# A hybrid attention trunk on one core: merge gates moved between the mixers, first output units interleaved, AV read in two places, one reciprocal a head, fillers at the start, new planner durations

## The chip, the core and the metric

The kernel runs on one core of a Trainium2 chip, in one launch. The metric is the time of one execution on the device in microseconds (us), here the median of three runs. Beside the times stands one profiled execution, a record of every instruction with its start, its length and what it waited for. Engines are named as in the profile: PE is TensorE (matmuls), PEld its weight loads, DVE is VectorE, ACT is ScalarE, POOL is GpSimd, SP is SyncE, which issues the DMAs. L407 is line 407 of the kernel before the change.

## The reference

x is [1, 256, 1024] in float32. Two layers follow each other, each of this form:

```
h = rms_norm(x) * gain
proj = h @ w_in                                  # 1024 -> 9808 columns, split into the parts below
oa = moba_attention(rope(qa), rope(ka), va)      # 8 heads of 64; 256 tokens are one block: causal attention
ob = dsa_attention(rope(qb), rope(kb), vb, ...)  # keeps the 64 best keys a query by an index score
oc = forgetting_attention(qc, kc, vc, log_f)     # causal, with a bias from the sums of log_f
o* = o* * silu(g*)                               # ga, gb, gc: 512 columns each
y  = [oa @ w_branch[0], ob @ w_branch[1], oc @ w_branch[2]]
merged = sum over branches of sigmoid(merge_logit) * y     # merge_logit: 3 x 1024 columns
x = x + merged @ w_out
```

The index score of the second branch is the sum over 8 heads of w * relu(q_idx . k_idx). After the layers comes one last RMS norm. Rotary embedding turns the first 16 of the 64 columns of a head.

## The kernel before, in words

**Precision.** Every float32 operand of a matmul is split into a high part (rounded to the fp32r format) and a low part, the rest. A product of two numbers then takes three matmuls: high by high, low by high, high by low. Weights come from DRAM in chunks of up to 1 MB (`raw`, 3 buffers) and are split in pieces of 128x1024: ACT writes the high part `wh` (L362), DVE the low part `wl` (L366), 6 buffers of each. Activations are split in the same way: `hTh`/`hTl` is the normalised, transposed input of a layer, `og0h`/`og0l` and `og1h`/`og1l` are gated branch outputs, `v` is the value operand and later, in the same space, the merged activations.

**Units.** The projections are cut into units, each with one bank of PSUM (`proj`, 3 banks). All their matmuls stand at L407. `unit_b` makes 128 output columns for all 256 tokens from 8 chunks of the input width: 24 matmuls of 256 moving columns. Two units in a row share one 1 MB chunk and its two split pieces. `unit_a` makes 128 tokens by 512 output columns: 24 matmuls of 512 moving columns (values, output projection); its weights are four pieces, `gets[0]` to `gets[3]`, each for two of the eight chunks. `unit_y` is the branch projection, 12 matmuls of 256; two units share one piece. Their names: q, g, k with branch letter and pair (`qa0`), `va0`, `vc0` for values, `qi0` to `qi3` for the index queries, `m20` for merge gate 0 of branch c (n = 0, 1, 2 are branches a, b, c), `y20` for its branch projection, `o00` to `o11` for the output projection (half of the columns, tile of tokens).

**Order of a layer.** Values of a, then the index key, then the index queries and mixer a, with merge gates between their units; values of c and mixer c with branch projections of a and merge gates; values of b and mixer b with branch projections of c and merge gates; the rest of b's merge gates; b's branch projections; the output projection. `between(main, fill)` spreads pairs of `fill` units evenly behind pairs of `main` units; `alternate(a, b)` takes pairs in turn. NC1 says how many of c's eight merge gates stand beside mixer a, NB1 how many of b's stand beside mixer b. All matmuls of units carry one token (`k_main`), so PE runs the units exactly in the written order.

**Attention.** A mixer has four pairs of heads. When a pair's q and k are done, `attend` runs: scores (6 matmuls, L574 to L576), for each head and each of the two query tiles a masked maximum (DVE, L637), an exponential with its sum (ACT, L641), a reciprocal of the sum (DVE, L645) and the normalising (DVE or ACT, L649/L652), then three transposes a head (L664), the split of the transposed weights (ACT L667, DVE L669) and AV, four matmuls a head (L679 to L682). AV's output goes through `gated` (ACT L695, DVE L697, product with the gate on DVE L700) and is split again (L397, L398). With the index scores done, `select` finds the 64 best keys by eight rounds of top-8 and replace on DVE (L808, L809).

**Token order.** Units read their moving operand in turns, one column from the first half of the tokens and one from the second (`turns`). Before the change AV reads its moving operand in plain order.

**Planner.** No engine's order is written by hand. At build time `Plan.run` simulates the five queues with a duration for each operation (`t_act`, `t_dve`, `t_pool`, `t_mm` and additions such as HALF) and delays between engines (LAG). It repeatedly takes the engine that can start next, and of the operations ready there the one with the lowest key. Keys are the numbers of the units, so that an earlier unit's work goes first; split pieces carry a key 2 lower than their unit (SPLIT_LEAD). The order so found is fixed in the program, and each engine runs its queue strictly in that order. Durations thus never change what is computed, only the order and which of two engines does an operation that has two ways.

**Start and end.** Fourteen matmuls of ones by ones (L870) run first on PE. `first_v` (L955) makes the values of a in layer 0, both tiles of tokens mixed, as the weights arrive. At the very end `forms` (L1048 to L1077) issues 28 matmuls whose results nobody reads, with several ways to read the moving operand.

Of the kernel before, what the change touches and what calls it, by code (L numbers as in the profile page):

```python
# [15 lines left out]
S = 256  # L16
# [23 lines left out]
HALF = 95.0  # L40
# [4 lines left out]
NC1 = 4  # L45
DMA_KEY = (-95, -94, -85, -84)
HI_KEY = (-60, -48, -47, -46)
NB1 = 2
# [186 lines left out]
def hybrid_trunk(ctx, tc, x, norm_gain, w_in, forget_bias, w_branch, w_out, final_gain, consts, out):  # L235
# [109 lines left out]
    def piece(key, ckey, ap, cshape, sel, shape, k):  # L345
# [21 lines left out]
        act(hi, a * b, False, [c], [p[0]], k - SPLIT_LEAD, f"hi {key}")  # L367
# [22 lines left out]
    def split_to(hi, lo, src, n, ps, reads, wh, wl, key, scale=None, name=""):  # L390

        if scale is None:
            act(lambda: ACT.activation(hi(), src(), AF.Copy), n, ps, reads, [wh], key, name)
            dve(lambda: DVE.tensor_tensor(lo(), src(), hi().bitcast(F32), op=ALU.subtract), n,
                reads + [wh], [wl], key, name, port=not ps)
        else:
            act(lambda: ACT.activation(hi(), src(), AF.Copy, scale=scale), n, ps, reads, [wh], key, name)  # L397
            dve(lambda: DVE.scalar_tensor_tensor(lo(), src(), scale, hi().bitcast(F32), op0=ALU.mult,  # L398
                                                 op1=ALU.subtract), n, reads + [wh], [wl], key, name, port=not ps)
# [35 lines left out]
    def unit_a(name, gets, t, ah, al, ra, c=0, n=512):  # L435
        u = unit(name)
        ps = Buf("proj")
        o = lambda: T(ps)[:, :n].rearrange("p (b a) -> p b a", a=2)
        for i in range(4):
# [11 lines left out]
    def rope(ps, which, key, np_=128):  # L451
# [3 lines left out]
        dve(lambda: DVE.stream_shuffle(T(sh)[:np_], a(), SWAP), S, [ps], [sh], key, "rope")  # L455
        gps(lambda: POOL.tensor_tensor(T(sh)[:np_], T(sh)[:np_], s[:np_], op=ALU.mult), S, [k_rope], [sh], key, "rope")  # L456
        dve(lambda: DVE.tensor_tensor(T(r)[:np_], a(), c[:np_], op=ALU.mult), S, [ps, k_rope], [r], key, "rope")
# [122 lines left out]
    class Pair:  # L580
# [46 lines left out]
        def attend(self, key):  # L627
# [3 lines left out]
            for h in range(2):  # L631
# [4 lines left out]
                for t, a, n, s in parts:  # L636
                    dve(lambda t=t, a=a, n=n, s=s, e=e, st=st, b=b, h=h: DVE.tensor_tensor_reduce(  # L637
                        T(e)[:, a:a + n], T(s)[:, :2 * n].rearrange("p (c h) -> p h c", h=2)[:, h], b()[:, a:a + n], 1.0, 3e38, ALU.add, ALU.min,
                        T(st)[:, t:t + 1]), n, [s, bt[t]], [kt[t]], key, "max", touch=[e, st] + bb)
                for t, a, n, s in parts:  # L640
                    act(lambda t=t, a=a, n=n, e=e, st=st: ACT.activation(  # L641
                        T(e)[:, a:a + n], T(e)[:, a:a + n], AF.Exp, bias=T(st)[:, t:t + 1], scale=-1.0,
                        accum_out=T(st)[:, 2 + t:3 + t]), n, False, [], [kt[t]], key, "exp", 185.0, touch=[e, st])
                for t, a, n, s in parts:
                    dve(lambda t=t, st=st: DVE.reciprocal(T(st)[:, 4 + t:5 + t], T(st)[:, 2 + t:3 + t]), 1, [], [kt[t]],  # L645
                        key, "recip", 75.0, touch=[st])
# [12 lines left out]
            for h in range(2):  # L659
# [5 lines left out]
                pe(tr, 330.0, ke[h] + [k_id], [ps], key, "pT", MARGIN, touch=[es[h]])  # L665
# [8 lines left out]
            def av():  # L674
                for h in range(2):
                    hd = 2 * self.p + h
                    ov = T(o)[:, h * S:(h + 1) * S]
                    a, b = slice(0, 256), slice(256, 384)
                    PE.matmul(ov, v[:, 0, hd], T(ph)[:, h, a], start=True, stop=False, skip_group_check=True)  # L679
# [4 lines left out]
            pe(av, 700.0, kv + [ph, pl] + [t for h in kp for t in h], [o], key, "av", MARGIN)  # L684
# [4 lines left out]
        def gated(self):  # L689
# [3 lines left out]
            for h in range(2):  # L693
                r = slice(64 * h, 64 * h + 64)
                act(lambda r=r, h=h: ACT.activation(T(t)[r], T(o)[64:, h * S:(h + 1) * S], AF.Copy), S, True,  # L695
                    [o], [kt[h]], key, "og", HALF, touch=[t])
                dve(lambda r=r, h=h: DVE.tensor_tensor(T(t)[r], T(o)[:64, h * S:(h + 1) * S], T(t)[r], op=ALU.add),  # L697
                    S, [o], [kt[h]], key, "og", t_dve(S) + HALF, touch=[t])
            plan.op([("POOL", t_pool(S), lambda: POOL.tensor_tensor(plain(T(t)), plain(T(t)), tiles(T(g)), op=ALU.mult)),
                     ("DVE", t_dve(S), lambda: DVE.tensor_tensor(plain(T(t)), plain(T(t)), tiles(T(g)), op=ALU.mult))],  # L700
                    [g] + kt, [t], key, 0.0, "og").port = True
            gh, gl = og[self.oi]
            split_to(lambda: gh[:, self.p], lambda: gl[:, self.p], lambda: T(t), S, False, [t],
                     k_og[self.oi][0][self.p], k_og[self.oi][1][self.p], key, 0.5, "og")

    def write_bd(src, b, toks, key, ps, shared=False):
        for h in range(2):
# [4 lines left out]
            act(lambda hi=hi, s=s: ACT.activation(hi(), s(), AF.Copy), S, ps, [src, k_bdz], [toks[h][0]], key, "bd", HALF, touch=[b])  # L712
            dve(lambda hi=hi, lo=lo, s=s: DVE.tensor_tensor(lo(), s(), hi().bitcast(F32), op=ALU.subtract), S,  # L713
                [src, toks[h][0]], [toks[h][1]], key, "bd", t_dve(S) + HALF, touch=[b], port=not ps)
# [8 lines left out]
    def wf_cols(l, key):  # L723
# [33 lines left out]
        dve(post, 0, [], [k_lf], key, "lf", 2500.0)  # L757
# [12 lines left out]
    def index_scores(p, ps, kb, ktoks, key):  # L770
# [8 lines left out]
        for h in range(2):  # L779
            hd = 2 * p + h  # L780
            for t, (a, n) in enumerate(((0, 128), (128, 256))):
# [7 lines left out]
                dve(f, n, [k_tmp[p % 2], k_widx], [k_isc[t]], key + 1, "isc", t_dve(n) + 61.0, port=True)  # L789
# [133 lines left out]
    def first_v():  # L923
# [36 lines left out]
        for t in range(2):  # L960
            v_out(ps[t], t, 0, done[t], us[t])

# [37 lines left out]
    for l in range(L):  # L1000
# [18 lines left out]
        for f in between(mixer(l, "c", 1, 1), alternate(y_of(l, 0, 0, 0, gates, range(8)), m_of(l, 2, gates, range(NC1, 8)))):  # L1019
            f()  # L1020
# [10 lines left out]
        for hh in range(2):  # L1031
            gets = [lambda k, i=i: rows_a("O", w_out, l, hh * 512, i, k) for i in range(4)]
            for t in range(2):
                ra = [lambda k, p=p: [k_mg[k][p]] for p in range(2)]
# [13 lines left out]
    def forms():  # L1048

        b = [Buf(t) for t in "sst"]  # L1050
        f = hTl.rearrange("p k c -> p (k c)")

        def emit():
            bs = [T(x) for x in b]
            n = 0

            def go(m, v, k):
                nonlocal n
                for i in range(k):
                    x = v(i)  # L1060
                    y = x.shape
                    o = bs[n % 3][:, :m]
                    if len(y) == 3:
                        o = o.rearrange("p (b a) -> p b a", a=y[2])
                    elif len(y) == 4:
                        o = o.rearrange("p (c b a) -> p c b a", b=y[2], a=y[3])
                    PE.matmul(o, hTh[:, i, :128], x, start=True, stop=True)
                n += 1
            go(256, lambda i: f[:, i * 256:i * 256 + 256].rearrange("p (c a b) -> p c b a", c=2, a=2), 4)
            go(256, lambda i: f[:, i * 64:i * 64 + 768].rearrange("p (a b) -> p b a", a=2)[:, :128], 4)  # L1070
            go(256, lambda i: f[:, i * 64:i * 64 + 1024].rearrange("p (a b) -> p b a", a=2)[:, :128], 4)
            go(256, lambda i: f[:, i * 256:i * 256 + 264].rearrange("p (a b) -> p b a", a=2)[:, :128], 4)
            go(256, lambda i: f[:, i * 256:i * 256 + 288].rearrange("p (a b) -> p b a", a=2)[:, :128], 4)
            go(512, lambda i: f[:, i * 64:i * 64 + 1024].rearrange("p (a b) -> p b a", a=2)[:, :256], 4)
            go(128, lambda i: f[:, i * 256:i * 256 + 128].rearrange("p (a b) -> p b a", a=2), 4)
# [29 lines left out]
```

## Time and profile before

| | us |
|---|---|
| median of 3 runs (lowest to highest) | 619.04 (618.86 to 620.8) |
| the profiled execution, its own time | 620.75 |
| its span, first to last instruction | 618.6 |
| PE busy | 606.7 (98%) |
| DVE busy | 540.0 (87%) |
| ACT busy | 407.0 (66%) |
| POOL busy | 82.2 (13%) |
| moved by DMA | 105.55 MB, mean 171 GB/s |

A stage is a stretch of the span. By the starts of their units, mixer a of layer 0 with its index units runs from 26 to 116.6 us, mixer c to 192.4, mixer b to 260, the rest of the merge gates and b's projections to 291.5, the output projection to 314.4. In layer 1 the same borders are at 329.1, 416, 491, 558.7, 590.2 and 612.4. A matmul's recorded length holds its pipeline's fill and drain, so that neighbours overlap; the distance from one start to the next says what it costs.

### The profile page before, as it was taken

How to read it: one execution, taken by the hardware profiler on the slowest of the kernel's cores; microseconds unless marked ns; L12 is line 12 of the kernel's file. 1: busy time of each engine (PE TensorE's matmuls, PEld its weight loads, DVE VectorE, ACT ScalarE, POOL GpSimd, SP SyncE). 2: the span in 40 equal slices, each digit the busy share in tenths (PEclk: the TensorE clock that was granted, in tenths of full speed). 3: DMA queues.
4: the chain of work that ended last, by engine and by line, in shares of the span. 5: the costliest groups of instructions: out<-in, count | busy, mean ns of one | idle time of the engine just before them, and what ended most of it. 6: DMA issues, size and time to landing. Idle time of an engine off the chain costs nothing.

```text
span 618.6 us, 12635 instructions
## 1 busy us (share of the span) xinstructions
PE 606.7 (98%) x4864; PEld 584.7 (95%) x4864; DVE 540.0 (87%) x1319; ACT 407.0 (66%) x814; POOL 82.2 (13%) x96
## 2 busy tenths in 40 slices
PE   7999999999999999999999999999999999999998
PEld 6999998999999999999789999999999999999987
DVE  8799999895979989999678999989688998999973
ACT  5676485775756658596386656868567675858741
POOL 1233130200000222200003412020000002311001
PEclk9999999999999999999999999999999999999999
DMA  8746537556374550836656446374645455363811
GB/s 297 252 138 198 167 114 229 157 178 222 103 244 133 171 188 25 266 127 215 202 159 204 132 142 204 119 256 155 208 150 177 130 161 182 103 209 103 304 34 69
DMA packets 93853, 105.55 MB, mean 171 GB/s; under 512 B 4321, under 2 KB 82401, under 8 KB 93793
## 3 DMA queue, kind: packets, MB, share of 16 engines
q1 hardware_dynamic: 93504, 104.36, 53.0%
q8 instruction: 38, 0.62, 0.4%
q10 hardware_dynamic: 288, 0.39, 0.2%
q14 instruction: 23, 0.18, 0.1%
HBM read 103.69 MB, written 1.05 MB: 169 GB/s over the span
## 4 chain that ended last, share of the span: by engine, by line
PE 70%; DVE 20%; ACT 1%; issue 1%; ACTq 0%; DVEq 0%
PE proj L407 60%; DVE wl L366 7%; PE t L664 2%; DVE isc L809 2%; DVE t L808 1%; PE s L574 1%; PE s L576 1%; PE s L575 1%; DVE e L637 1%; DVE mth L856 1%; DVE acc L858 1%; DVE v L398 1%; PE o L679 1%; PE o L682 1%; ACT wh L362 1%
## 5 line engine op out<-in xcount | busy, mean ns | idle before, releaser
L366 DVE TENSOR_TENSOR wl<-raw,wh 128x1024 fp32r<-128x1024 f32 (+1 forms) x190 | 236.2, 1254 | 30.3 <-ACT wh L362 28.7
L407 PE MATMUL proj<-hTh,wh 128*128 128x256 f32 (+1 forms) x1040 | 246.8, 276 | 0.8 <-DVE bd0l L713 0.8
L407 PE MATMUL proj<-hTl,wh 128*128 128x256 f32 (+1 forms) x1040 | 245.6, 275 | 0.0
L362 ACT ACTIVATE wh<-raw 128x1024 fp32r<-128x1024 f32 (+1 forms) x190 | 198.1, 1055 | 69.5 <-PE proj L407 49.2
L407 PEld LDWEIGHTS proj<-hTh,wh 128*128 128x128 f32 (+1 forms) x1040 | 198.9, 191 | 1.3 <-DVE bd0l L713 1.0
L407 PEld LDWEIGHTS proj<-hTl,wh 128*128 128x128 f32 (+1 forms) x1040 | 198.9, 191 | 0.4
L407 PE MATMUL proj<-hTh,wl 128*128 128x256 f32 (+1 forms) x1040 | 160.3, 277 | 2.3 <-DVE wl L366 2.3
L407 PEld LDWEIGHTS proj<-hTh,wl 128*128 128x128 f32 (+1 forms) x1040 | 138.0, 191 | 4.0 <-DVE wl L366 3.1
L456 POOL TENSOR_TENSOR rsh<-rsh,cst 128x256 f32<-128x256 f32 (+1 forms) x42 | 33.5, 796 | 403.5 <-DVE rsh L455 401.9
L641 ACT ACTIVATE e<-e,st 128x128 f32<-128x128 f32 x96 | 42.7, 446 | 10.9 <-DVE st L637 10.9
L458 POOL TENSOR_TENSOR rr<-rr,rsh 128x256 f32<-128x256 f32 (+1 forms) x42 | 43.4, 1034 | 8.5 <-ACT wh L362 2.5
L407 PE MATMUL proj<-wh,v 128*128 128x512 f32 (+1 forms) x144 | 34.8, 359 | 1.3 <-DVE v L398 0.9
L407 PE MATMUL proj<-og0h,wh 128*128 128x256 f32 x128 | 32.0, 276 | 0.0
L407 PE MATMUL proj<-og0l,wh 128*128 128x256 f32 x128 | 31.9, 275 | 0.0
L407 PE MATMUL proj<-wh,hTh 128*128 128x512 f32 x80 | 31.4, 392 | 0.1
L407 PE MATMUL proj<-wh,hTl 128*128 128x512 f32 x80 | 30.4, 380 | 0.2 <-DVE hTl L522 0.2
L407 PEld LDWEIGHTS proj<-wh,v 128*128 128x128 f32 x144 | 25.2, 190 | 5.5 <-DVE v L398 1.5
L695 ACT ACTIVATE ot<-o 64x256 f32<-64x256 f32 x48 | 18.3, 381 | 14.0 <-PE o L682 13.3
L669 DVE TENSOR_TENSOR ptl<-t,pth 128x384 fp32r<-128x384 f32 x48 | 25.4, 552 | 0.3 <-ACT pth L667 0.2
L407 PE MATMUL proj<-og0h,wl 128*128 128x256 f32 x128 | 24.8, 275 | 0.0
L407 PEld LDWEIGHTS proj<-og0l,wh 128*128 128x128 f32 x128 | 24.6, 192 | 0.0
L407 PEld LDWEIGHTS proj<-og0h,wh 128*128 128x128 f32 x128 | 24.6, 192 | 0.0
(194 smaller groups left out, 1025.5 us busy)
## 6 DMA issues: line engine op xcount, KB each, us to landing
raw<-in_w_in_dram SPq DMA_DIRECT2D x74, 1024.0 KB, 5.2
raw<-in_w_branch_dram SPq DMA_DIRECT2D x24, 512.0 KB, 4.7
raw<-in_w_out_dram SPq DMA_DIRECT2D x8, 1024.0 KB, 5.4
raw<-in_w_in_dram SPq DMA_DIRECT2D x3, 512.0 KB, 7.2
x<-in_x_dram SPq DMA_DIRECT2D x4, 256.0 KB, 4.9
raw<-in_w_in_dram SPq DMA_DIRECT2D x2, 320.0 KB, 6.9
out_dram<-tmp SPq DMA_DIRECT2D x2, 320.0 KB, 2.5
raw<-in_w_in_dram SPq DMA_DIRECT2D x2, 256.0 KB, 3.9
```

Of the source, the lines that this page charges most:

```text
L362: ACT.activation(p[0].v, sel(c.v), AF.Copy)
L366: DVE.tensor_tensor(p[1].v, sel(c.v), p[0].v.bitcast(F32), op=ALU.subtract)
L398: dve(lambda: DVE.scalar_tensor_tensor(lo(), src(), scale, hi().bitcast(F32), op0=ALU.mult, op1=ALU.subtract), n, reads + [wh], [wl], key, ...
L407: PE.matmul(o(), a(), b(), start=first and i == 0, stop=last and i == n - 1)
L456: gps(lambda: POOL.tensor_tensor(T(sh)[:np_], T(sh)[:np_], s[:np_], op=ALU.mult), S, [k_rope], [sh], key, "rope")
L458: gps(lambda: POOL.tensor_tensor(T(r)[:np_], T(r)[:np_], T(sh)[:np_], op=ALU.add), S, [sh], [r], key, "rope")
L574: PE.matmul(o, qh[:, sl], mh, start=True, stop=False)
L641: act(lambda t=t, a=a, n=n, e=e, st=st: ACT.activation(T(e)[:, a:a + n], T(e)[:, a:a + n], AF.Exp, bias=T(st)[:, t:t + 1], scale=-1.0, acc ...
L664: PE.transpose(T(ps)[:, i * 128:(i + 1) * 128], T(es[h])[:, i * 128:(i + 1) * 128], ident)
L669: dve(lambda h=h, src=src: DVE.tensor_tensor(T(pl)[:, h], src(), T(ph)[:, h].bitcast(F32), op=ALU.subtract), 384, [ps, kp[h][0]], [kp[h][1 ...
L695: act(lambda r=r, h=h: ACT.activation(T(t)[r], T(o)[64:, h * S:(h + 1) * S], AF.Copy), S, True, [o], [kt[h]], key, "og", HALF, touch=[t])
L809: dve(lambda o=o, t8=t8: DVE.match_replace(o, T(t8), o, TAKEN), n, [t8], [k_isc[i]], key + r * step, "top8")
```

## The change

What it does, part by part:

1. NC1 goes from 4 to 8: all eight merge gates of c stand beside mixer a, none beside mixer c. NB1 goes from 2 to 0: all eight of b's stand behind mixer b.
2. `unit_a2` makes the first two output units, o00 and o01, in turns: three quarters of o00, three quarters of o01, the last quarter of o00, the last of o01.
3. AV reads its moving operand in turns of two places 64 tokens apart within a tile of 128, so its output has another order of tokens; `gated` reads the gate in that order, and the split of the gated output puts the tokens back. The factor 0.5 moves from the split into the two operations before.
4. One reciprocal a head takes both tiles' sums, 48 instructions of 128x2 for 96 of 128x1.
5. Ten matmuls of ones by ones, with the lowest urgency, may run on PE once the first matmul of `first_v` is done. `forms` is gone.
6. The planner's durations change: HALF 95 to 113, a split piece on ACT +18 ns, splits from SBUF on ACT +72 and on DVE +26, three transposes 330 to 275, AV 700 to 696, and others by a few ns.

```diff
-HALF = 95.0
+HALF = 113.0
-NC1 = 4
+NC1 = 8
-NB1 = 2
+NB1 = 0
...
-        act(hi, a * b, False, [c], [p[0]], k - SPLIT_LEAD, f"hi {key}")
+        act(hi, a * b, False, [c], [p[0]], k - SPLIT_LEAD, f"hi {key}", 18.0)
...
     def split_to(hi, lo, src, n, ps, reads, wh, wl, key, scale=None, name=""):
+        ea, ed = (0.0, 10.0) if ps else (72.0, 26.0)
+        if name == "og":
+            ea = 16.0
...
+    def unit_a2(name, gets, ah, al, ra):
+        us = [unit(f"{name}{t}") for t in range(2)]
+        ps = [Buf("proj") for _ in range(2)]
+        for t, q in ((0, (0, 1, 2)), (1, (0, 1, 2)), (0, (3,)), (1, (3,))):
+            unit_a(f"{name}{t}", gets, t, ah, al, ra, part=(us[t], ps[t], q))
+        return list(zip(us, ps))
+
+    def unit_a(name, gets, t, ah, al, ra, c=0, n=512, part=None):
+        u, ps, q = part or (unit(name), Buf("proj"), range(4))
...
+                dve(lambda st=st: DVE.reciprocal(T(st)[:, 4:6], T(st)[:, 2:4]), 2, [], kt, key, "recip", 75.0, touch=[st])
                 for t, a, n, s in parts:
-                    dve(lambda t=t, st=st: DVE.reciprocal(T(st)[:, 4 + t:5 + t], T(st)[:, 2 + t:3 + t]), 1, [], [kt[t]],
-                        key, "recip", 75.0, touch=[st])
...
-                pe(tr, 330.0, ke[h] + [k_id], [ps], key, "pT", MARGIN, touch=[es[h]])
+                pe(tr, 275.0, ke[h] + [k_id], [ps], key, "pT", MARGIN, touch=[es[h]])
...
-                    a, b = slice(0, 256), slice(256, 384)
-                    PE.matmul(ov, v[:, 0, hd], T(ph)[:, h, a], start=True, stop=False, skip_group_check=True)
-                    PE.matmul(ov[:, 128:], v[:, 1, hd], T(ph)[:, h, b], start=False, stop=True, skip_group_check=True)
-                    PE.matmul(ov[:64, 128:], v[:, 1, hd, :64], T(pl)[:, h, b], start=False, stop=False, skip_group_check=True)
-                    PE.matmul(ov[:64], v[:, 0, hd, :64], T(pl)[:, h, a], start=False, stop=True, skip_group_check=True)
+                    f = lambda x, t: turns(x[:, h, 256:]) if t else x[:, h, :256].rearrange("p (t a b) -> p t b a", t=2, a=2)
+                    o0 = lambda r: ov[:r].rearrange("p (t b a) -> p t b a", t=2, a=2)
+                    o1 = lambda r: ov[:r, 128:].rearrange("p (b a) -> p b a", a=2)
+                    PE.matmul(o0(128), v[:, 0, hd], f(T(ph), 0), start=True, stop=False, skip_group_check=True)
+                    PE.matmul(o1(128), v[:, 1, hd], f(T(ph), 1), start=False, stop=True, skip_group_check=True)
+                    PE.matmul(o1(64), v[:, 1, hd, :64], f(T(pl), 1), start=False, stop=False, skip_group_check=True)
+                    PE.matmul(o0(64), v[:, 0, hd, :64], f(T(pl), 0), start=False, stop=True, skip_group_check=True)
...
-                dve(lambda r=r, h=h: DVE.tensor_tensor(T(t)[r], T(o)[:64, h * S:(h + 1) * S], T(t)[r], op=ALU.add),
+                dve(lambda r=r, h=h: DVE.scalar_tensor_tensor(T(t)[r], T(o)[:64, h * S:(h + 1) * S], 0.5, T(t)[r], op0=ALU.mult, op1=ALU.add),
...
+            def gate():
+                tv = T(t).rearrange("p (t b a) -> p t b a", t=2, a=2)
+                return tv, tv, T(g).rearrange("p (a b t) -> p t b a", a=2, t=2)
...
+            nat = lambda x: x.rearrange("p (t a b) -> p t a b", t=2, a=2)
+            split_to(lambda: nat(gh[:, self.p]), lambda: nat(gl[:, self.p]), lambda: T(t).rearrange("p (t b a) -> p t a b", t=2, a=2), S, False, [t],
+                     k_og[self.oi][0][self.p], k_og[self.oi][1][self.p], key, name="og")
...
+        idle = Buf("o")
+        for i in range(10):
+            pe(lambda: PE.matmul(T(idle)[:, :128], ones, ones, start=True, stop=True), 215.0, done[0][:1], [idle], 10 ** 5, "warm")
...
+            pair = unit_a2("o0", gets, mA[0], mA[1], ra) if hh == 0 else None
...
-                    u, ps = unit_a(f"o{hh}{t}", gets, t, mA[0], mA[1], ra, c, n)
+                    u, ps = pair[t] if pair else unit_a(f"o{hh}{t}", gets, t, mA[0], mA[1], ra, c, n)
...
-    def forms():
...
-    forms()
```

More of the change, by code (lines that the diff above doesn't have):

```diff
@@ L390, in split_to @@
     def split_to(hi, lo, src, n, ps, reads, wh, wl, key, scale=None, name=""):
+        ea, ed = (0.0, 10.0) if ps else (72.0, 26.0)
+        if name == "og":
+            ea = 16.0
         if scale is None:
-            act(lambda: ACT.activation(hi(), src(), AF.Copy), n, ps, reads, [wh], key, name)
+            act(lambda: ACT.activation(hi(), src(), AF.Copy), n, ps, reads, [wh], key, name, ea)
             dve(lambda: DVE.tensor_tensor(lo(), src(), hi().bitcast(F32), op=ALU.subtract), n,
-                reads + [wh], [wl], key, name, port=not ps)
+                reads + [wh], [wl], key, name, t_dve(n) + ed, port=not ps)
         else:
-            act(lambda: ACT.activation(hi(), src(), AF.Copy, scale=scale), n, ps, reads, [wh], key, name)
+            act(lambda: ACT.activation(hi(), src(), AF.Copy, scale=scale), n, ps, reads, [wh], key, name, ea)
             dve(lambda: DVE.scalar_tensor_tensor(lo(), src(), scale, hi().bitcast(F32), op0=ALU.mult,
-                                                 op1=ALU.subtract), n, reads + [wh], [wl], key, name, port=not ps)
+                                                 op1=ALU.subtract), n, reads + [wh], [wl], key, name, t_dve(n) + ed, port=not ps)
     def mm_ops(o, terms, cost, writes, key, name, first, last, main=False):
@@ L433, in unit_b @@
         return u, ps
-    def unit_a(name, gets, t, ah, al, ra, c=0, n=512):
-        u = unit(name)
-        ps = Buf("proj")
+    def unit_a2(name, gets, ah, al, ra):
[6 more added lines that the diff above has]
+        u, ps, q = part or (unit(name), Buf("proj"), range(4))
         o = lambda: T(ps)[:, :n].rearrange("p (b a) -> p b a", a=2)
-        for i in range(4):
+        for i in q:
             p = gets[i](u)
@@ L711, in write_bd @@
             lo = lambda o=o, h=h: plain(T(b)[1][o, h])
-            act(lambda hi=hi, s=s: ACT.activation(hi(), s(), AF.Copy), S, ps, [src, k_bdz], [toks[h][0]], key, "bd", HALF, touch=[b])
+            act(lambda hi=hi, s=s: ACT.activation(hi(), s(), AF.Copy), S, ps, [src, k_bdz], [toks[h][0]], key, "bd", HALF + (0.0 if ps else 104.0), touch=[b])
             dve(lambda hi=hi, lo=lo, s=s: DVE.tensor_tensor(lo(), s(), hi().bitcast(F32), op=ALU.subtract), S,
-                [src, toks[h][0]], [toks[h][1]], key, "bd", t_dve(S) + HALF, touch=[b], port=not ps)
+                [src, toks[h][0]], [toks[h][1]], key, "bd", t_dve(S) + HALF + 15.0, touch=[b], port=not ps)
     def ev_kwf(l, ps, key):
@@ L756, in post @@
             DVE.scalar_tensor_tensor(lf, z, 0.0, u, op0=ALU.min, op1=ALU.subtract)
-        dve(post, 0, [], [k_lf], key, "lf", 2500.0)
+        dve(post, 0, [], [k_lf], key, "lf", 2700.0)
         cs = Buf("t")
@@ L788, in index_scores @@
                     f = lambda rr=rr, w=w, o=o: DVE.scalar_tensor_tensor(o, rr, w, o, op0=ALU.mult, op1=ALU.add)
-                dve(f, n, [k_tmp[p % 2], k_widx], [k_isc[t]], key + 1, "isc", t_dve(n) + 61.0, port=True)
+                dve(f, n, [k_tmp[p % 2], k_widx], [k_isc[t]], key + 1, "isc", t_dve(n) + 76.0, port=True)
     def select(key, step):
@@ L1018, in hybrid_trunk @@
         v_units(l, "c", 1)
-        for f in between(mixer(l, "c", 1, 1), alternate(y_of(l, 0, 0, 0, gates, range(8)), m_of(l, 2, gates, range(NC1, 8)))):
+        for f in between(mixer(l, "c", 1, 1), alternate(m_of(l, 2, gates, range(NC1, 8)), y_of(l, 0, 0, 0, gates, range(8)))):
             f()
@@ L1047, in hybrid_trunk @@
                     norm_to_hT(l + 1, t, u - 2)
-    def forms():
[L1050 to L1075, printed above, removed]
-        pe(emit, 4000.0, [k_main] + hT_all[0] + hT_all[1], b, 10 ** 6, "forms")
-    forms()
     PLAN_T.append(plan)
```

20 lines of the change are left out of this document (9 added, 11 removed).

## The prediction

> **What bounds it now.** I read the page first: which engine is busy, and the chain that ended last.
>
> ```profile
> span 618.6 us, 12635 instructions
> PE 606.7 (98%) x4864; PEld 584.7 (95%) x4864; DVE 540.0 (87%) x1319; ACT 407.0 (66%) x814; POOL 82.2 (13%) x96
> PE 70%; DVE 20%; ACT 1%; issue 1%; ACTq 0%; DVEq 0%
> ```
>
> PE looks full, but the chain goes through DVE for a fifth of the span: there PE waits in small pieces, which the modelled ends of its matmuls cover. So I count starts. Chain pieces give the distances:
>
> ```profile
> 207.30 0.13 PE o L679
> ...
> 207.67 0.12 PE o L679
> ...
> 208.03 20.10 PE proj L407 x180
> ...
> 612.39 0.89 PE s L1067 x8
> 613.29 0.45 PE t L1067 x4
> ...
> 614.63 0.87 PE t L1067 x4
> ```
>
> A projection matmul of 256 columns costs 20.10/180 = 0.112 us, one of 512 0.87/4 = 0.22. The same taken over all starts (each form's usual distance as floor, what exceeds it as stall) gives a floor of 591 us and 23.3 us of stall. Now by stage, two layers each, the last two rows parts of a stage:
>
> ```profile
> core 0: us, PE busy (x) PEld busy (x) DVE busy (x) ACT busy (x) POOL busy (x), PEclk, DMA share, GB/s
> 26.00:116.60 90.60, 87.72 (x752) 85.44 (x751) 86.53 (x227) 59.06 (x111) 24.87 (x26) 1.00 0.54 169
> 329.10:416.00 86.90, 86.33 (x751) 84.99 (x750) 81.76 (x214) 58.72 (x107) 23.79 (x26) 1.00 0.54 171
> 116.60:192.40 75.80, 75.04 (x623) 73.14 (x622) 62.79 (x149) 51.49 (x110) 0.00 (x0) 1.00 0.57 181
> 416.00:491.00 75.00, 75.00 (x623) 73.11 (x622) 62.73 (x155) 52.07 (x115) 0.00 (x0) 1.00 0.55 176
> 192.40:260.00 67.60, 67.60 (x560) 65.84 (x559) 61.66 (x152) 43.53 (x87) 13.59 (x16) 1.00 0.50 156
> 260.00:291.50 31.50, 31.50 (x282) 31.29 (x281) 29.57 (x76) 26.00 (x57) 0.48 (x1) 1.00 0.55 185
> ...
> 59.00:75.80 16.80, 16.15 (x144) 15.96 (x144) 16.80 (x56) 8.22 (x12) 1.08 (x2) 1.00 0.64 191
> 206.20:232.00 25.80, 25.80 (x231) 25.69 (x231) 23.43 (x51) 14.55 (x28) 7.06 (x8) 1.00 0.68 215
> ```
>
> Floor and stall by my count: mixer a 85.2 + 5.4 in layer 0 and 85.0 + 1.9 in layer 1 (the same matmuls take 3.7 us longer, which the two rows show without any model); mixer c 74.1 + 1.9 and 73.9 + 1.1; mixer b 66.6 + 0.7 and 66.9 + 0.8; the rest of the gates with b's projections 31.2 + 0.3 and 31.2 + 0.4; the first output units 1.3 and 1.1. Beside these stand 7.4 us up to 26 us. In layer 0's mixer a DVE has 86.5 us of work for 85.2 of PE's: it is the bound there (16.80 of 16.80 us in its middle), and all long waits of PE for a split weight fall there:
>
> ```profile
> PEld proj L407 <- DVE wl L366: 3.1, 3, 1.6
> PE proj L407 <- DVE wl L366: 2.3, 3, 1.4
> ```
>
> In mixers c and b PE is the bound, DVE at 83% and 91%.
>
> **The change, part by part.** The sum is made against the profiled execution's own 620.75 us (span 618.6 and 2.15 around it); the median of the runs shown, 619.04, lies 1.71 lower, and the forecast is set down by that.
>
> *forms goes.* The rows of the tail:
>
> ```profile
> 614.88 0.34 SPq L561 DMA_DIRECT2D out_dram<-tmp  x1
> 615.33 0.56 PE L1067 MATMUL s<-hTl,hTh 128*128 128x128 f32 x4
> out_dram<-tmp SPq DMA_DIRECT2D x2, 320.0 KB, 2.5
> ```
>
> They end at 615.89; the last store goes out at 614.88 and lands 2.5 us later, at 617.4. The 28 matmuls lie under DVE's and ACT's final norm and the store: 0. Without that cover they would cost 3.5.
>
> *AV.* A head takes 0.37 us (207.30 to 207.67, and 0.36 to 208.03). forms holds the new reading at the very shapes: the first eight rows at 612.39 begin with four in two places, 0.111 us each. With two of 256 and two of half that a head costs 0.33. 48 heads by 0.03 to 0.04: 1.4 to 1.7 by rounded rows; the medians of the starts (0.357) give 1.0. I take **-1.2**, bounds -1.7 and -0.7.
>
> *Reciprocals, gating, splits, on DVE.*
>
> ```profile
> L366 DVE TENSOR_TENSOR wl<-raw,wh 128x1024 fp32r<-128x1024 f32 x188 | 234.5, 1258 | 30.3 <-ACT wh L362 28.7 <-PE proj L407 0.2
> L394 DVE TENSOR_TENSOR ql<-rr,qh 128x256 fp32r<-128x256 f32 x24 | 11.0, 471 | 0.4 <-ACT qh L393 0.3
> L645 DVE RECIPROCAL st<-st 128x1 f32<-128x1 f32 x96 | 13.7, 155 | 0.8 <-ACT e L641 0.4
> L398 DVE SCALAR_TENSOR_TENSOR og0l<-ot,og0h 128x256 fp32r<-128x256 f32 x16 | 6.7, 421 | 1.1 <-ACT og0h L397 1.1
> L858 DVE TENSOR_TENSOR acc<-acc,mth 128x256 f32<-128x256 f32 x32 | 12.9, 420 | 0.1
> L856 DVE SCALAR_TENSOR_TENSOR mth<-mth,proj 128x256 f32<-128x256 f32 x32 | 12.8, 416 | 0.1
> ```
>
> 48 fewer reciprocals save 48 x 0.155 = 7.4 us of DVE; a second column is under 0.01 each. The split of the gated output now reads in turns, as L394 does: at worst 24 x (471 - 421) = 1.2 us more. Net 6 us, 1.0 a mixer. The joined reciprocal waits for the second tile's exponential; behind it on DVE stand both normalisings and whatever the planner put later, and the transposes wait. But these read both tiles anyway, so the path loses at most one normalising, and pairs are units ahead of AV: 0 on the path.
>
> *Gates to mixer a (NC1).* Four gate units bring 4 x 24 x 0.112 = 10.7 us of PE and, as two units share two `wl`, 4 x 1.26 = 5.0 us of DVE, with two 1 MB loads on SP's queue (DMA share 0.54 there). PE 85.2 + 10.7 = 95.9, DVE 86.5 + 5.0 - 1.0 = 90.5: from 102% of PE to 94%. Layer 1: 81.8 + 4.0 = 85.8 on 95.7, 90%. Moreover k0 k1 q2 q3, which stood in a row without a gate between, get two, and there the backlog peaked. Layer 1's 94% had 1.9 us of stall, so layer 0 goes from 5.4 to about 2.2, **-3.2** (bounds 0: the stall follows the 64-key selection wherever it stands; -4.5), layer 1 from 1.9 to 0.9, **-1.0** (0; -1.7).
>
> *Mixer c* loses those: PE 74.1 - 10.7 = 63.4, DVE 62.8 - 5.0 - 1.0 = 56.8, 90% where it was 85%. **0** (-1.0; +1.5 for both layers): such a share stood in mixer b with 0.7 of stall.
>
> *Mixer b* loses two gates: PE 66.6 - 5.4 = 61.2, DVE 61.7 - 2.5 - 1.0 = 58.2, 95%. Its first part (206.2 to 232) falls to 20.4 of PE against 23.43 - 2.5 - 0.5 = 20.4 of DVE: even. Splits run two units ahead, 5.4 us, which takes up a short backlog. I take **+1.4** for both layers (0.7 to 1.4 each), bounds 0 and +6.
>
> *End of a layer.* The two gates come behind mixer b: PE 36.6, DVE 32, 88% where it was 94%. And o00 no longer waits for the last merged channels:
>
> ```profile
> 594.24 1.14 DVE wl L366
> 595.37 0.34 DVE v L398
> 595.72 0.04 issue
> 595.76 16.63 PE proj L407 x99
> ```
>
> Here DVE's row of splits and merges ends at 595.7 with PE idle. The three quarters of o01 are 18 x 0.22 = 3.9 us of work that needs none of it; both edits aim at the same 1.3 + 1.1 us, and a little of the 0.7 before. **-2.2** (-2.7; -1.0). Three `proj` banks suffice: y15 and y16 are read out by then.
>
> *Start.* Windows of the first matmuls:
>
> ```profile
> 8.00:10.00 2.00, 1.60 (x9) 1.05 (x6) 2.00 (x8) 2.00 (x8) 0.00 (x0) 1.00 1.03 364
> 10.00:11.00 1.00, 0.00 (x0) 0.00 (x0) 1.00 (x4) 1.00 (x3) 0.00 (x0) 1.00 1.06 414
> ...
> 13.00:14.00 1.00, 1.00 (x4) 0.82 (x3) 1.00 (x2) 1.00 (x2) 0.00 (x0) 0.50 1.14 317
> 14.00:15.00 1.00, 1.00 (x4) 0.73 (x3) 0.80 (x3) 0.63 (x1) 0.00 (x0) 0.50 1.07 323
> 15.00:16.00 1.00, 1.00 (x6) 0.90 (x5) 0.89 (x1) 0.23 (x1) 0.00 (x0) 0.50 1.09 360
> 16.00:18.00 2.00, 2.00 (x12) 1.79 (x12) 1.53 (x6) 1.97 (x8) 0.00 (x0) 0.95 1.05 325
> ```
>
> PE idles about 1.7 us, and from 13 to 16 the granted clock is 0.50. At full clock that work (14 matmuls in 3 us) would take half, 1.5 us less. Ten fillers of 0.21 (the planner's 215 ns) are 2.1 us, the size of the gap. If they hold the clock, DVE and the loads behind it (DMA share 1.05) give back perhaps two thirds: **-1.2**; -2.0 if all of it and a bit of the gap; +1.0 if five fillers stand in front of work that is ready.
>
> By the Trainium skill, TensorE: Matmul & The Clock Gate, The HAM clock gate, the clock halves after an idle window of about 3.4 us and returns after as long a busy one, the windows running free of the program. The slow stretch here, about 3.3 us, agrees; the gap of 1.7 us is only half of such a window, so by the page the gap alone need not be the cause, and the fillers' term could be 0. The sum would then be -6.2 instead of -7.4.
>
> *Durations.* They change order only. A split on ACT is planned at 947 ns and measured at 1.06 us median; +18 goes the right way; three transposes at 330 against 0.33 us with their drain. I give them 0, inside the bounds above.
>
> Sum: -1.2 - 3.2 - 1.0 + 0 + 1.4 - 2.2 - 1.2 = **-7.4**: 620.75 - 7.4 = 613.35, on the median's footing **611.6 us**.
>
> **The rivals.**
>
> *Half of it (614 to 617).* The gates move but the stall stays: selection still goes before splits by its key, and each gate brings DVE work. Then mixer a gives 1.0 in all and the start nothing: -1.2 - 1.0 + 1.4 - 2.2 = -3.0, 616.0. For it: the DVE share of layer 0 stays at 94%. Against: layer 1 shows 1.9 at that share.
>
> *No change: mixer b gives it back.* PE waits there for splits as it did in 75.8 to 116.6 of layer 0, where it lost some 10%: 4.8 us a layer on 48 us, 9.6 in place of 1.4. -7.4 + 8.2 = +0.8, 619.8.
>
> *Slower: too few gates between the pairs.* One mechanism in two places: without gates, mixers b and c have stretches where evictions, pairs of heads and branch projections load DVE above PE. It decides once the backlog exceeds the two units' lead, 5.4 us; then PE waits at that 10% in b (48 us) and in the later half of c (32.5 - 5.4 = 27 us): 4.8 + 2.7 a layer, 15.0 together instead of 1.4. -7.4 + 13.6 = +6.2, **625.2**. For it: the even balance in the first part of b, and c's branch projections, which cost DVE 1.26/2 + 0.42 + 0.42 = 1.47 a unit (L366, L856, L858) and PE 12 x 0.112 = 1.34. Against: c keeps 10% in hand.
>
> *More.* Mixer a falls to its floor in both layers, the start gives all: -4.5 - 1.7 - 2.0 - 1.7 - 2.7 + 1.4 = -11.2, 607.8.
>
> *A part does not do what it says.* The planner may put the fillers elsewhere; that is within the start's bounds.
>
> **How the numbers follow.** Forecast 50% (609 to 614), half 22%, no change 10%, slower 12%, more 6%. A measurement here can't tell under 0.3%, 1.9 us, from no change. Faster is forecast, half and more: 0.78; same 0.10; slower 0.12. The range goes from 606.5, a little beyond the most, to 619.5, which leaves out the slower case and part of the no-change case.
>
> **What would show it.** Right: in mixer a's stage of layer 0 no wait of PE for L366 over 0.5 us and a stage of 97 to 99 us (90.6 + 10.7 - 3.2), 96 to 97 in layer 1; no wait for L398 before o00's last quarter; granted clock 1.00 from 13 to 16 us; L645 48 times; AV at 0.33 a head. Wrong: waits of PE for L366 in the stages of mixer b or c, or a DVE busy throughout there; a filler that ends after the weights it stood before had arrived.

## The result and the profile after

The changed kernel takes 609.31 us (median of 4 runs, 609.16 to 609.97), the kernel before 618.95 us: a ratio of 0.984, interval 0.982 to 0.986, 9.6 us or 1.6% less. The forecast was 611.6 with a range of 606.5 to 619.5. One execution of the kernel with the gates alone, below, took 1602.84 us and is left out of that kernel's ratio.

The page of the profiled execution, from the lines that answer to those of before:

```profile
span 607.4 us, 12561 instructions
PE 599.1 (99%) x4856; PEld 580.8 (96%) x4856; DVE 537.9 (89%) x1270; ACT 406.8 (67%) x811; POOL 85.7 (14%) x100
PE 88%; DVE 9%; issue 1%; ACT 1%; DMA 0%; POOL 0%; POOLq 0%; DVEq 0%
```

The chain that ended last runs through PE for 88% of the span, where it was 70%; DVE's share of it fell from 20% to 9%, although DVE does nearly the same work. (A second profile of the kernel before, further down, shows 73% and 18%.) These are all the waits of PE's matmuls over 0.15 us in the whole execution; the first is that of the matmuls of ones that open it. The columns are the sum in us, how often, and the longest:

```profile
PE t L885 <- DVE ones L881: 1.1, 1, 1.1
PE s L586 <- DVE bd2l L728: 0.5, 1, 0.5
PE proj L410 <- DVE hTl L532: 0.2, 1, 0.2
```

No wait of that length for a weight split (L366) and none for the merged split is left. Short ones must be left, since the chain still goes through L366 for 3% of the span, nearly all of it in the two mixers a. By windows, each cut from the first matmul of a stage to the first of the next (mixer a, mixer c, mixer b, gates and projections behind it, output projection, all of layer 0, then mixer a of layer 1):

```profile
core 0: us, PE busy (x) PEld busy (x) DVE busy (x) ACT busy (x) POOL busy (x), PEclk, DMA share, GB/s
23.95:121.09 97.14, 97.03 (x848) 95.87 (x847) 91.49 (x226) 65.60 (x121) 23.31 (x26) 1.00 0.60 191
121.09:184.96 63.87, 63.87 (x526) 62.01 (x525) 56.34 (x136) 46.11 (x101) 0.81 (x1) 1.00 0.52 166
184.96:246.94 61.98, 61.98 (x513) 60.26 (x512) 57.94 (x139) 41.06 (x84) 15.13 (x17) 1.00 0.46 145
246.94:283.73 36.79, 36.79 (x330) 36.63 (x329) 33.99 (x77) 28.06 (x60) 0.57 (x1) 1.00 0.60 201
283.73:305.33 21.60, 21.60 (x106) 18.98 (x105) 15.38 (x21) 12.37 (x22) 0.55 (x1) 1.00 0.52 162
319.93:417.45 97.52, 96.90 (x848) 95.78 (x847) 88.09 (x226) 63.17 (x115) 22.89 (x26) 1.00 0.57 179
```

DVE's work in layer 0's mixer a is 91.5 us beside 97.1 us of stage, in mixer b 57.9 beside 62.0: 94% and 93%, close to the predicted 90.5 and 58.2. Four gate units are 96 x 0.112 = 10.7 us of PE; with these added, mixer a of layer 0 would have taken 90.6 + 10.7 = 101.3 us by the old rate, and takes 97.1. Layer 1's would have taken 97.8 and takes 97.5.

### The profile page after: what moved, and what is told of

Its sections match the earlier page's. It is cut to its first block, busy times and chain, and to the rows that moved or that the text cites. A ratio compares the mean times of both kernels' runs of the same rounds, so it can differ in the third digit from the quotient of the medians.

```text
span 607.4 us, 12561 instructions
## 1 busy us (share of the span) xinstructions
PE 599.1 (99%) x4856; PEld 580.8 (96%) x4856; DVE 537.9 (89%) x1270; ACT 406.8 (67%) x811; POOL 85.7 (14%) x100
## 4 chain that ended last, share of the span: by engine, by line
PE 88%; DVE 9%; issue 1%; ACT 1%; DMA 0%; POOL 0%; POOLq 0%; DVEq 0%
PE proj L410 74%; DVE wl L366 3%; PE t L673 3%; PE proj L970 2%; PE s L586 2%; PE s L585 2%; PE s L584 2%; PE o L690 1%; PE o L693 1%; DVE isc L824 1%; DVE t L823 1%; PE t L629 1%; DVE isc L803 1%; DVE rsh L465 1%; PE o L692 0%
## 5 line engine op out<-in xcount | busy, mean ns | idle before, releaser
L366 DVE TENSOR_TENSOR wl<-raw,wh 128x1024 fp32r<-128x1024 f32 (+1 forms) x190 | 237.1, 1257 | 24.2 <-ACT wh L362 22.6
L410 PE MATMUL proj<-og0h,wl 128*128 128x256 f32 x128 | 24.7, 275 | 0.0
```

The costliest lines, as they stand in the source:

```text
L366: DVE.tensor_tensor(p[1].v, sel(c.v), p[0].v.bitcast(F32), op=ALU.subtract)
L410: PE.matmul(o(), a(), b(), start=first and i == 0, stop=last and i == n - 1)
```

## The experiments

Twelve runs follow, each timed against the kernel before on the same chip; one of them is that kernel itself. Its median differs from one set of timings to the next by up to 0.5 us (618.95 to 619.47), and the changed kernel stands in one set only, so differences of that size between two runs of different sets say little. To compare stages I use the lengths from each stage's first unit to the next stage's. "Shifted" is the kernel before with the units that NC1 and NB1 move counted in their new stage, at 0.112 us a matmul; the second profile of the kernel before (its own section below) stands for it. "a0" is mixer a of layer 0, "end" the gates and projections behind mixer b, "o" the output projection; "start" is where a0 begins.

| us | start | a0 | c0 | b0 | end 0 | o0 | a1 | c1 | b1 | end 1 | o1 | time |
|---|---|---|---|---|---|---|---|---|---|---|---|---|
| before, shifted | 24.3 | 101.3 | 65.0 | 62.4 | 36.9 | 22.9 | 97.8 | 64.2 | 62.2 | 36.9 | 22.0 | 618.95 |
| gates alone | 24.5 | 98.8 | 64.3 | 62.4 | 36.9 | 21.6 | 97.3 | 64.3 | 62.4 | 36.9 | 20.8 | 613.30 |
| gates and durations | 24.2 | 97.1 | 64.0 | 62.4 | 36.9 | 21.6 | 98.1 | 64.0 | 62.4 | 36.9 | 20.8 | 611.32 |
| all | 24.0 | 97.1 | 63.9 | 62.0 | 36.8 | 21.6 | 97.5 | 63.9 | 62.0 | 36.8 | 20.8 | 609.31 |
| all, old durations | 24.3 | 98.5 | 64.0 | 63.3 | 37.9 | 21.6 | 96.6 | 64.0 | 63.3 | 38.0 | 20.8 | 615.63 |

### The gates put back

```diff
-NC1 = 8
+NC1 = 4
-NB1 = 0
+NB1 = 2
```

Besides, mixer c's fill takes its turns as in the kernel before.

> The changed kernel, with the gates where they stood before (NC1 4, NB1 2, and the fill of mixer c in its former turns); all else as changed. Theory A (moving the gates rebalances mixer a): about 4 us slower than the changed kernel, 613 us; layer 0's mixer a has 4 to 5 us of stall again, DVE busy throughout its middle, and mixers c and b gain nothing. Theory B (the new durations gave the better order): within 1 us of 609.3, layer 0's mixer a with under 2 us of stall.

Measured: 619.41 us, ratio to the kernel before 1.0006 (0.9995 to 1.0016). Without the moved gates nothing of the gain is left, which is far more than theory A allowed. The matmuls' waits:

```profile
PE proj L410 <- DVE wl L366: 1.7, 3, 0.7
...
PE proj L410 <- DVE og0l L397: 1.0, 1, 1.0
PE proj L410 <- ACT og0h L396: 0.8, 1, 0.8
```

The waits for splits are back, in mixer a of layer 0 (90.3 us for the same units that took 90.6). New is the wait for the gated output `og0h` and `og0l`: y00, the first branch projection of a, comes only two q units behind the values of c and finds the last pair of mixer a unfinished. Mixer c of layer 0 takes 77.5 us, 1.8 more than before the change, at the old order of units. So the other parts together are worth nothing here, and something among them costs; the durations alone, below, show the same wait in the same place.

### Without the fillers

```diff
-        for i in range(10):
+        for i in range(0):
```

> The changed kernel without the ten fillers. Theory A (they hold the clock and the start is worth it): 1.7 us slower, 611.0 us, granted clock 0.50 again for about 3 us after 12.5 us, units after the start 1.5 to 2 us later. Theory B (the gap of 1.7 us is not the cause of the slow clock, or mixer a takes the lead back): within 0.5 us of 609.3.

Measured: 609.82 us (609.65 to 611.18), 0.5 above the changed kernel's median; the index queries begin at 24.5 us, within the 24.0 to 24.7 of the runs with fillers. The granted clock did not fall:

```profile
12.00:14.00 2.00, 1.44 (x7) 1.19 (x7) 1.67 (x2) 1.85 (x3) 1.03 (x1) 1.00 1.11 327
14.00:16.00 2.00, 2.00 (x15) 1.78 (x13) 1.80 (x4) 2.00 (x7) 0.00 (x0) 1.00 1.05 336
```

Theory B holds for this execution: the gap of 1.7 us is there, and the clock stays at 1.00. A difference of 0.5 us is at the limit of what these timings tell.

### Without the interleaved output units

```diff
-            pair = unit_a2("o0", gets, mA[0], mA[1], ra) if hh == 0 else None
+            pair = unit_a2("o0", gets, mA[0], mA[1], ra) if False else None
```

> The changed kernel with o00 and o01 one after the other. Theory A (the interleaved quarters hide the wait for the last merged channels): 2.0 to 2.4 us slower, 611.5 us, waits of PE for the merged split before o00's last quarter of 1.1 us in each layer. Theory B (more gates behind mixer b already leave DVE ahead, so the wait is gone anyway): within 0.5 us of 609.3.

Measured: 609.40 us, 0.1 above the changed kernel. Theory B: the gates behind mixer b alone remove the wait before o00's last quarter. The run with the gates put back has the interleaving and no such wait either (21.6 and 20.8 us in its output stages); but so does the run with the durations alone (21.7 and 20.9 us), which has neither the interleaving nor the moved gates. So the moved gates suffice, and the interleaving adds nothing to them; whether it would do by itself was not tried.

### With the old durations

```diff
-HALF = 113.0
+HALF = 95.0
...
-        act(hi, a * b, False, [c], [p[0]], k - SPLIT_LEAD, f"hi {key}", 18.0)
+        act(hi, a * b, False, [c], [p[0]], k - SPLIT_LEAD, f"hi {key}")
...
-        ea, ed = (0.0, 10.0) if ps else (72.0, 26.0)
+        ea, ed = 0.0, 0.0
```

And so with every other duration of the change.

> The changed kernel with every duration of the planner as before. Theory A (durations only reorder): within 1 us of 609.3, either side. Theory B (they carry much of the gain): 612 us or more, with new waits of PE in mixer a, c or b.

Measured: 615.63 us, 6.3 above the changed kernel; theory B. In the table the loss is 1.4 us in mixer a of layer 0, 1.3 in each mixer b, 1.1 to 1.2 in each end of a layer, with 0.9 gained in mixer a of layer 1. The weight loads of the transposes, first here, then in the changed kernel (last columns: idle time before them, and for whom):

```profile
L673 PEld LDWEIGHTS t<-cst,e 128*128 128x128 f32 x144 | 16.6, 140 | 4.7 <-ACT e L658 2.9 <-DVE e L661 0.4
```

```profile
L673 PEld LDWEIGHTS t<-cst,e 128*128 128x128 f32 x144 | 16.8, 141 | 2.0 <-DVE e L661 0.3
```

By the old durations PE comes to the transposes before ACT has normalised, 2.9 us in all in waits over 0.15 us, and not once by the new ones. That is under half of the 6.3 us. In mixer b of layer 0 the chain now runs through DVE and ACT from 221.8 us on, until at 251.8 the scores of a pair get their split k from DVE, just after the stage's end; in the changed kernel it stays on PE there. The new durations are the distances from one start to the next that the trace of before shows where instructions follow closely: a split on ACT 0.965 us median of 109 (planned 0.947, now 0.965), the split of k from SBUF on ACT 0.521 of 29 (planned 0.402, now 0.524), of q on DVE 0.358 of 24 (0.335, now 0.361). That ACT runs behind the old plan is shown for this set of parts; which of the durations it is was not separated. With two reciprocals a head and the same old durations (below) that wait is 1.0 us, so it is not the durations' alone.

### The gates alone

```diff
-NC1 = 4
+NC1 = 8
-NB1 = 2
+NB1 = 0
```

> The kernel before with NC1 8 and NB1 0 and nothing else. After the first four runs (gates put back: the whole gain gone; old durations: two thirds of it gone). Theory A (the moved gates and the new durations need each other): 616 to 617.5 us, mixer a of layer 0 at about 98.5 us, mixer b with 1 to 2 us of stall a layer, end of a layer without its wait. Theory B (the gates alone carry the gain): 610 to 611 us.

Measured: 613.30 us, ratio 0.990 (0.9875 to 0.9924): 5.7 to 6.2 us less than before, between the two theories. Mixer a and mixer b of layer 0 and its output projection:

```profile
24.54:123.38 98.84, 97.57 (x849) 95.97 (x847) 92.97 (x234) 65.22 (x122) 24.93 (x26) 1.00 0.58 187
...
187.70:250.09 62.39, 62.39 (x513) 60.48 (x511) 58.00 (x146) 42.35 (x86) 17.68 (x18) 1.00 0.45 146
...
286.97:308.57 21.60, 21.60 (x107) 18.98 (x106) 15.32 (x24) 11.88 (x21) 0.55 (x1) 1.00 0.51 162
```

Against the shifted stages: -2.5 in mixer a of layer 0, -0.5 in layer 1, -0.7 and +0.1 in mixer c, 0 and +0.2 in mixer b, -1.3 and -1.2 in the output projections, which have no interleaving here. DVE has 58.0 us of work in mixer b's 62.4, and the stage is no longer than the shifted one.

### The old AV

```diff
-                    PE.matmul(o0(128), v[:, 0, hd], f(T(ph), 0), start=True, stop=False, skip_group_check=True)
+                    PE.matmul(ov, v[:, 0, hd], T(ph)[:, h, a], start=True, stop=False, skip_group_check=True)
```

So for the other three matmuls; the gating and the split of its output are the old ones too.

> The changed kernel with AV reading in plain order, the old gating and the old split of the gated output. Theory A (PE is the bound and each start counts): 0.8 to 1.2 us slower, 610.1 to 610.5 us, a head of AV at 0.36 us again. Theory B (the gap is hidden, or the dearer strided split costs as much): within 0.4 us of 609.3.

Measured: 610.48 us, 1.2 above the changed kernel: theory A, the whole of the term. By the profiles the stages behind the start lose 0.8 us, and the start, which scatters by 0.8 us among the runs with fillers, another 0.5. Pieces of the chain in the changed kernel show a pair's AV:

```profile
201.13 0.11 PE o L690
...
201.47 0.11 PE o L690
...
201.81 20.55 PE proj L410 x184
```

A head takes 0.34 us, where it took 0.36 to 0.37. Over 24 pairs the medians are 0.680 and 0.723 us, 1.0 us together. The price on the other engines is larger than forecast, as ACT pays too, and the run gives no sign that it costs anything here (the changed kernel's groups):

```profile
L396 ACT ACTIVATE og0h<-ot 128x256 fp32r<-128x256 f32 x16 | 7.9, 496 | 6.1 <-DVE ot L714 6.0
L397 DVE TENSOR_TENSOR og0l<-ot,og0h 128x256 fp32r<-128x256 f32 x16 | 7.3, 458 | 1.1 <-ACT og0h L396 1.1
L654 DVE RECIPROCAL st<-st 128x2 f32<-128x2 f32 x48 | 6.6, 156 | 2.1 <-ACT e L651 1.9
```

### The durations alone

The kernel before with all new durations and without the 28 matmuls at its end.

```diff
-HALF = 95.0
+HALF = 113.0
```

> The kernel before with the new durations alone (and without the 28 matmuls at the end). Theory A (they need the moved gates): 619 to 621 us, no gain. Theory B (they are worth 6 us by themselves): 612.5 to 614 us.

Measured: 625.21 us, ratio 1.0088 (1.0059 to 1.0116): 5.7 us slower, which no theory had. Not all of that is the order of work: the profiled execution took 622.77 us, 3.3 more than the median before, and the other three (624.5 to 626.3) show a mean granted clock of 0.991 to 0.996 beside its 0.999; where it fell in them is not recorded. In the profile the gates and projections behind mixer b take 33.9 us instead of 31.5, in both layers:

```profile
259.34:293.23 33.89, 32.05 (x282) 31.51 (x281) 30.60 (x80) 24.16 (x53) 0.49 (x1) 1.00 0.51 173
```

The chain at that place, in order of time, shows what they wait for:

```profile
278.40 0.14 PE o L692
...
278.57 0.38 ACT ot L705
...
278.96 0.38 ACT ot L705
...
279.36 1.06 ACT wh L362
...
280.45 0.38 ACT mth L835
...
280.83 0.95 ACT wh L362
...
281.81 1.22 DVE wl L366
...
283.03 0.35 DVE og0l L401
...
283.42 0.60 PE proj L410 x3
```

The last pair's AV ends at 278.5. Its read-out follows on ACT, then ACT splits a weight piece, makes a gate, splits another, and only then the gated output; DVE puts one more split of weights before its part. b's first branch projection, with six gate units before it as cover, waits for it: y10 loses 2.3 us. In the second profile of the kernel before, that pair's AV begins at 275.28 where it begins at 277.64 here, and y10 does not wait. With the gates moved, eight units stand in between. The two mixers c lose another 1.5 and 0.8 us, in layer 0 partly at y00, which waits 0.9 us for the gated output of mixer a; the output projections gain 1.2 and 1.1.

### The kernel before once more

> The kernel before once more, for a second profile. Theory A (the first profile's start was its own): the first unit of the index queries at 24.3 to 24.8 us instead of 26.05, span 617 us, all later stages as in the first profile within 0.3 us. Theory B (the slow start belongs to the kernel): 26 us again.

Nothing is edited. Measured: a span of 617.0 us; the index queries begin at 24.30 us instead of 26.05, and every later stage agrees with the first profile within 0.1 us. Theory A. Here too the granted clock stays at full speed:

```profile
12.00:14.00 2.00, 1.59 (x8) 1.30 (x8) 1.66 (x3) 1.86 (x3) 0.86 (x1) 1.00 1.10 342
14.00:16.00 2.00, 2.00 (x15) 1.80 (x14) 1.81 (x4) 2.00 (x8) 0.00 (x0) 1.00 1.10 339
```

So the half clock on which the start's term rested is not in every execution. It is hardly in that one alone either: of 29 more timings of this kernel, 7 show a mean granted clock of 0.994 or 0.997 and took 620.1 to 622.9 us, the other 22 show 0.999 or 1.000 and took 619.6 at most. The profiled execution of before had 0.997. Where the clock fell in the seven is not recorded.

### Gates and durations together

The moved gates and the new durations on the kernel before, without AV, the joined reciprocal, the interleaving, the fillers and the 28 matmuls at the end. The diff is against the kernel before.

```diff
-HALF = 95.0
+HALF = 113.0
-NC1 = 4
+NC1 = 8
-NB1 = 2
+NB1 = 0
```

> The moved gates and the new durations alone, without the new AV, the joined reciprocal, the interleaved units and the fillers (and without the 28 matmuls at the end). So far: gates alone 613.3, durations alone 625.2, the changed kernel 609.3. Theory A (with the gates moved the durations pay by themselves): 610.5 to 611.5 us, and AV with 1.2 and the fillers with 0.5 make up the rest to 609.3. Theory B (they only mend what the other parts do to the order): 613 us or more.

Measured: 611.32 us, ratio 0.9874 (0.9847 to 0.9902). Theory A: the durations, which cost with the gates in their old places, gain 2.0 with the gates moved (1.6 by the two ratios, whose intervals overlap). Part of it lies again before the transposes, here in the gates alone and then with the durations:

```profile
L664 PEld LDWEIGHTS t<-cst,e 128*128 128x128 f32 x144 | 16.7, 141 | 3.8 <-DVE e L652 1.5 <-ACT e L649 0.9
```

```profile
L674 PEld LDWEIGHTS t<-cst,e 128*128 128x128 f32 x144 | 16.9, 140 | 2.5 <-DVE e L662 0.8
```

### A reciprocal for each tile

```diff
-                dve(lambda st=st: DVE.reciprocal(T(st)[:, 4:6], T(st)[:, 2:4]), 2, [], kt, key, "recip", 75.0, touch=[st])
                 for t, a, n, s in parts:
+                    dve(lambda t=t, st=st: DVE.reciprocal(T(st)[:, 4 + t:5 + t], T(st)[:, 2 + t:3 + t]), 1, [], [kt[t]],
+                        key, "recip", 75.0, touch=[st])
```

> The changed kernel with a reciprocal for each tile of a head, 96 instead of 48. Theory A (DVE is not the bound any more, the saved 7 us are in its idle time): within 0.5 us of 609.3. Theory B (DVE at 94 per cent of PE's work in mixers a and b still decides): 1 to 2.5 us slower, with waits of PE for splits in mixer a of layer 0.

Measured: 611.11 us, 1.8 above the changed kernel: the size of theory B, though not its place. Mixer a of layer 0 is the same (97.0 us); 0.6 us lie in mixer a of layer 1, 0.3 in each mixer b, 0.25 in each end of a layer, 0.4 at the start, which is within its scatter, and PE never waits over 0.15 us for a weight split.

### Old durations and a reciprocal for each tile

The old durations and a reciprocal for each tile, both on the changed kernel.

```diff
-HALF = 113.0
+HALF = 95.0
...
-                dve(lambda st=st: DVE.reciprocal(T(st)[:, 4:6], T(st)[:, 2:4]), 2, [], kt, key, "recip", 75.0, touch=[st])
```

> The changed kernel with the old durations and with a reciprocal for each tile: the gates, AV, interleaved units and fillers by the old plan. It tells why the old durations with all parts (615.6) are slower than the gates alone by the same durations (613.3). Theory A (the joined reciprocal upsets the old plan): 611.5 to 612.5 us. Theory B (the new AV with its dearer gating upsets it, or the order is simply another draw): 615 us or more.

Measured: 612.82 us, nearer to theory A. By the old plan the joined reciprocal costs 2.8 us (615.63 against 612.82), by the new one it gains 1.8. The same edit saves or adds 7 us of DVE work either way, so its sign must come from something else; the order that comes out of the plan is what is left, though no single place was found.

### Three more durations

```diff
-            ea = 16.0
+            ea = 97.0
...
-                    [o], [kt[h]], key, "og", HALF, touch=[t])
+                    [o], [kt[h]], key, "og", HALF + 20.0, touch=[t])
...
-                     ("DVE", t_dve(S), lambda: DVE.tensor_tensor(*gate(), op=ALU.mult))],
+                     ("DVE", t_dve(S) + 72.0, lambda: DVE.tensor_tensor(*gate(), op=ALU.mult))],
```

> The changed kernel with three more durations set to the distances of its own trace: the product with the gate +72 ns, the split of the gated output on ACT +81, the read-out of AV on ACT +20. Theory A (what helps is a plan that is not too fast, so more of it helps or does nothing): 608.5 to 609.5 us. Theory B (the order is a draw, and any change of a duration moves the time by microseconds either way): outside 608 to 611 us.

Measured: 609.98 us, 0.7 above the changed kernel: just outside what theory A gave, and well within the 608 to 611 us that theory B said it would leave. So neither theory holds as put. Setting three more durations to the trace's distances brought nothing; no version tried is faster than the changed kernel.

## Why the prediction held, and where its steps failed

The total was about right (-7.4 forecast, -9.6 measured between the medians), and the main mechanism too. That the number came so near is partly luck: terms that were wrong, some too large and some too small, offset each other.

- **Bound and cure: right.** Layer 0's mixer a was held up by DVE, and moving gate units into it relieved it. For the gates with the end of the layer the terms were -3.2 - 1.0 + 0 + 1.4 - 2.2 = -5.0; the gates alone measured -5.7. Stage by stage they fit less well: the mixers a gave -2.5 and -0.5, where -3.2 and -1.0 were forecast, and the mixers b cost 0.2 instead of 1.4. In the whole change the mixers a gain 4.2 and 0.3; layer 1's 97.5 us lie outside the 96 to 97 that were named as a sign. Without the gates the change gains nothing.
- **Mixers c and b: the sign of one term was wrong.** The step "I take +1.4 for both layers", drawn from DVE at 95% of PE's work, measured +0.2 in the gates alone, and -0.6 in the whole change. A DVE share of 93% cost PE nothing there; that no backlog outlived the two units' lead is the likely reason, not a measured one. By the old durations with all other parts the same share came with a loss of 1.3 us in each mixer b, so the share alone does not set the price. The slower rival did not come about: in none of the kernels with moved gates does a matmul wait over 0.15 us for L366 in mixer b or c.
- **End of a layer: right in size, wrong in cause.** The output projections gained 1.3 and 1.2 us, about as forecast, but the gates alone bring all of it; the interleaving was worth 0.1, which is no more than scatter.
- **AV: right.** -1.2 forecast, 1.2 measured by leaving it out, 1.0 by starts. The rows of the 28 matmuls at the end did price it. The dearer split was put at 1.2 us of DVE at worst; ACT's part, 417 to 496 ns, was missed, and no cost of it is seen.
- **Start: wrong.** -1.2 forecast from a stretch of half clock that one execution had; the fillers measured 0.5 in the medians and nothing beyond the scatter of the starts in the traces. The step that failed is to take one profile's start for the kernel's, and the sum counted it twice: the 1.71 us by which the profiled execution lay above the median are that same start (1.75 us between the two profiles), so with the forecast set down to the median the term had nothing left to save. Without it the sum gives 612.8 us; that the double count and the surplus of 1.2 in mixer b cancel is luck. The rule set against it, that the gate looks at windows of about 3.4 us running free of the program (the Trainium skill, TensorE: Matmul & The Clock Gate, The HAM clock gate), agrees with what came: of six profiles without fillers that have this gap, one fell to 0.50, and its slow stretch was 3.4 us (12.8 to 16.2).
- **Durations: the step that failed most.** "I give them 0, inside the bounds above." They are worth -2.0 with the gates moved, -6.3 with all other parts present, and +5.7 alone (+3.3 in the profiled execution, whose clock did not fall). The same paragraph read 1.06 us as the cost of a split on ACT; that is the recorded length, and 0.965 the distance between starts, which the new duration meets exactly. The difference, 0.09 us, agrees with the Trainium skill (ScalarE: Activation LUTs, What ACT_TABLE_LOAD costs), by which activations that follow closely overlap by about 93 ns.
- **The joined reciprocal: "0 on the path" was wrong** by 1.8 us (about 1.5 of it behind the start); the saved DVE time was as forecast (13.7 to 6.6 us). That it works by way of the order is argued from the other sign under the old plan, not seen at a place.
- **The 28 matmuls at the end: not tried by themselves.** The stretch behind the last real matmul is 6.5 us with and without them, which agrees with 0.

The parts do not add. On top of gates and durations, AV, reciprocal, fillers and interleaving gain 2.0 us together, while left out one by one they cost 1.2, 1.8, 0.5 and 0.1. Each edit makes the planner write another order, and the order carries a part of the price. Why a given order comes out better was seen at two places only (the split of the gated output queued behind weight splits, and the transposes that come before the normalising is done); for the rest it stays open.

## What to carry to other kernels

Where a second engine holds up PE in one stage and not in the next, look for work that is heavy on PE and light on that engine, and move it there; price it from both stages' windows. In a kernel whose order is planned at build time, a duration is a change of the program: measure it as the distance from start to start, and test it together with the units' order, since the same numbers gained 2 us in one order and lost 3 to 6 in the other. Look at a second profile, and at the granted clock of all timed executions, before explaining the first microseconds of one; and when a sum starts from a profiled execution and ends at the median, see that what sets the two apart is not also a term of the sum.

## What the runs showed of the hardware

The granted clock fell to 0.50 for about 3.4 us after the same early gap of PE in one of six profiled executions without fillers, and in none of eight with them; with one case out of six that is no proof that fillers prevent it. The timings say that such falls are common: about a quarter of those of the kernel before (7 of 29) have a lower mean granted clock and take 1 to 4 us more. The kernel with the gates put back, which has the fillers, shows it too: two of its ten executions have 0.995 where the others have 0.997 or 0.998, and take 620.5 and 620.9 us beside 620.0 at most. And an AV matmul that reads 256 contiguous columns starts the next one after 0.118 to 0.120 us (medians over 48), one that reads them in turns after 0.112: the order of reading alone was worth 1.0 us over 24 pairs.
